# A hybrid attention layer on one core: the pace of the branch merges, a PSUM bank of the scan, and the order of the output phase

## The chip, the cores and the metric

The kernel runs on one core of one Trainium2 chip. The metric is the device time of one execution in microseconds; of several executions the median counts. The kernel before was timed three times: 2359.21, 2356.31 and 2359.18 us, median 2359.18 us. The five engines are named as in the profile: PE (TensorE, matmul), DVE (VectorE), ACT (ScalarE), POOL (GpSimd) and SP (SyncE, which here issues nearly all DMAs).

## The reference

One decoder layer for 2048 tokens of width 1024 in float32. The input is normalised and projected to 9224 columns. Branch A is a gated delta rule with 4 heads of 128 and chunks of 64; branch B is windowed attention in three groups of 4 heads, merged by the softmax denominators. Both are gated, projected back, mixed, multiplied by `w_out`, and x is added. Cut to what the change touches:

```python
tmat = lax.linalg.triangular_solve(eye + lower, ..., left_side=True, lower=True, unit_diagonal=True)
...
def step(S, inp):                      # scan over the 32 chunks, 4 heads
    v_new = ui - einsum('bhck,bhkv->bhcv', wi, S)
    o = einsum('bhck,bhkv->bhcv', qi * exp(gci), S) + einsum('bhij,bhjv->bhiv', ai, v_new)
    S = S * exp(glast) + einsum('bhck,bhcv->bhkv', ki * exp(glast - gci), v_new)
    return S, o
...
alpha = jax.nn.softmax(jnp.stack(lses, axis=0), axis=0)     # over the three groups
o_swa = jnp.sum(alpha[..., None] * jnp.stack(outs, axis=0), axis=0)
...
merged = sigmoid(g_dn) * y_dn + sigmoid(g_swa) * y_swa
x = x + merged @ w_out[layer]
```

## The kernel before

Large matmuls are done in float32 precision from two halves: each operand is split into a high part and a low remainder (`split`, L89 to L91: the high part on ACT, the remainder on DVE or POOL), and three products are added in one PSUM tile. Many of them are also done by a scheme of seven products for a 2x2 block product (`PROD`), for which sums of blocks are formed first.

The stages follow each other on PE. First comes the projection for the attention branch with the attention itself in its gaps. Then `cunits` (L710) runs 36 units of 128 output columns each, four tiles of 512 tokens to a unit, every tile 24 matmuls of 512 columns. Its units are three z units (branch A's gate), twelve units of the delta rule's q, k and v, twelve g units (the mixing gates, L1158), five z units (L1149) and four g units. Beside these units the delta rule's serial work is done:

- `inverse` (L1000) inverts 128 triangular 64x64 blocks at once, one block to a partition. Row i needs all rows before it: a product of i x i elements (L1023), two memsets, and a sum over the last axis (L1026), all on DVE. It starts in the first g unit.
- `combine` merges the three attention groups, 128 tokens at a time, 16 times (L1251). One merge is: a load of 128 x 1560 floats into an `oc` buffer; a minimum (L1260) and a difference (L1261) on DVE; an exp on ACT (L1262); four small operations on DVE (L1265 to L1268); three products of 512 columns on DVE (L1271); two additions on POOL (L1276); and a DMA to `osd` (L1278).
- `scan` (L1031) begins 20 steps after the inverse has ended. For each of 16 pairs of chunks it runs three stages for the heads 0, 1 (g = 0) and 2, 3 (g = 1). Stage 2 multiplies keys by new values into the tile `p4` (L1099 to L1101), from which DVE updates the states S (L1103).

After `cunits` come the branch projections and the mixing (`fin_y`, eight blocks of 256 tokens with eight tiles each), which writes `mscr`, and last the output phase: `group` (L1388), eight times, multiplies 256 tokens by `w_out` in seven products of 12 matmuls. Around them stand the loads of x (`x_load`), the holding of partial sums (`keep`, L1400 on ACT and L1402 on DVE), additions of x on POOL (`plus`, L1405), results with their DMA out (`result`, L1408 and L1409), and, for the operand four products ahead, loads from `mscr` (`m_load`, L1355), block sums (L1376) and splits (`m_op`).

Work that stands beside matmuls is placed by a clock of steps: `self.at(delay, fn)` puts a function on a list, and `hook()`, called after every second k (six matmuls of 512 columns in `cunits`, some 1.4 us), advances the clock by one and runs what is due. This sets the order in the program's source. What order an engine really gets is up to a planner: in a stretch under `pinned(False)` PE, ACT, DVE and POOL keep the source order and SP's is planned; under `pinned(True)` SP keeps it too; from the inverse's start to the end of `cunits` only PE keeps it; and in the output phase of the kernel before the planner orders all engines. Each engine runs its own queue strictly in the order it was given, and an instruction that waits holds up those behind it.

On-chip memory is drawn from pools, and a tile with `bufs=n` turns through n buffers: a new tile waits until the oldest one's users are done. PSUM has eight banks in these stages: three `mm`, two `tp`, two `sc`, one `po`. In the scan, stage 0 takes an `sc` tile for each pair of heads, the preparation of the next chunks two more, stage 1 a `tp` tile each, stage 2 the `po` tile twice. The gate tiles `gt` have two buffers in `cunits`, and a g tile is read out by ACT (L1161) and written to memory, a z tile by ACT (L1152) and DVE (L1153).

## Time and profile before

| What | Before |
|---|---|
| Median of 3 runs (lowest to highest) | 2359.18 us (2356.31 to 2359.21) |
| The profiled execution: its own time, its span | 2355.83 us, 2353.8 us |
| Granted TensorE clock, mean | 0.993 |
| PE, DVE, ACT, POOL busy | 2275.0, 1435.6, 919.8, 941.2 us |
| The inverse on DVE, from its first product to row 63's end | 1421.2 to 1694.8 us |
| First matmul of the scan | 1766.2 us |
| Output phase on PE | 2188.9 to 2350.0 us |

The profile is of one execution. Its span reaches from the first to the last instruction; the time of an execution has a little more around it (here 2.0 us). A row of a group names a source line, an engine, an operation, what it writes and reads, how often it ran, the busy time and mean duration, and the idle time just before it with the releaser of that wait. A row of the timeline gives start and duration in us. A row of the list of waits says which engine waited where, for whom, and then the total in us, the number of times and the longest.

### The profile page before, as it was taken

How to read it: one execution, taken by the hardware profiler on the slowest of the kernel's cores; microseconds unless marked ns; L12 is line 12 of the kernel's file. 1: busy time of each engine (PE TensorE's matmuls, PEld its weight loads, DVE VectorE, ACT ScalarE, POOL GpSimd, SP SyncE). 2: the span in 40 equal slices, each digit the busy share in tenths (PEclk: the TensorE clock that was granted, in tenths of full speed). 3: DMA queues.
4: the chain of work that ended last, by engine and by line, in shares of the span. 5: the costliest groups of instructions: out<-in, count | busy, mean ns of one | idle time of the engine just before them, and what ended most of it. 6: DMA issues, size and time to landing. Idle time of an engine off the chain costs nothing. (4 is left out here: it accounts for less than half of the span.)

```text
span 2353.8 us, 43662 instructions
## 1 busy us (share of the span) xinstructions
PE 2275.0 (97%) x15120; PEld 2063.3 (88%) x15120; DVE 1435.6 (61%) x2980; ACT 919.8 (39%) x2959; POOL 941.2 (40%) x1299
## 2 busy tenths in 40 slices
PE   7999999989999999999999999999999999999999
PEld 7999999889999999888788888777788888999787
DVE  6566586694445545446777768999813443666653
ACT  5345466653434435444666651111113333211221
POOL 6374265575303303303675563334212332332543
PEclk9999999999999999999999999999999999999999
DMA  9989889857887888853554445444345657787752
GB/s 304 325 279 322 276 276 292 271 160 247 259 258 239 250 272 262 257 145 98 127 131 123 117 108 181 144 127 134 126 143 164 196 170 229 232 277 240 249 157 89
DMA packets 557267, 485.80 MB, mean 206 GB/s; under 512 B 68280, under 2 KB 517112, under 8 KB 554104
## 3 DMA queue, kind: packets, MB, share of 16 engines
q1 hardware_dynamic: 556760, 482.95, 66.7%
q8 instruction: 120, 1.97, 0.3%
q14 instruction: 99, 0.81, 0.1%
q10 hardware_dynamic: 288, 0.07, 0.0%
HBM read 280.23 MB, written 202.67 MB: 205 GB/s over the span
## 5 line engine op out<-in xcount | busy, mean ns | idle before, releaser
L723 PE MATMUL mm<-hh,w 128*128 128x512 f32 x1152 | 465.2, 404 | 13.2 <-ACT gt L1161 9.8
L725 PE MATMUL mm<-hh,w 128*128 128x512 f32 x1152 | 458.2, 398 | 0.0
L724 PE MATMUL mm<-hl,w 128*128 128x512 f32 x1152 | 457.6, 397 | 0.0
L436 PE MATMUL mm<-w,hh 128*128 128x256 f32 x1760 | 326.8, 285 | 0.0
L723 PEld LDWEIGHTS mm<-hh,w 128*128 128x128 f32 x1152 | 220.8, 192 | 62.3 <-ACT gt L1161 12.9
L436 PEld LDWEIGHTS mm<-w,hh 128*128 128x128 f32 x1760 | 270.2, 189 | 0.0
L725 PEld LDWEIGHTS mm<-hh,w 128*128 128x128 f32 x1152 | 217.4, 189 | 46.9
L436 PE MATMUL mm<-hh 128*128 128x256 f32 x880 | 257.5, 293 | 0.0
L724 PEld LDWEIGHTS mm<-hl,w 128*128 128x128 f32 x1152 | 218.1, 189 | 41.9
L436 PE MATMUL mm<-hl,hh 128*128 128x256 f32 x880 | 249.7, 284 | 0.5 <-POOL hl L298 0.5
L436 PE MATMUL mm<-hh,hl 128*128 128x256 f32 x880 | 249.6, 284 | 0.0
L436 PE MATMUL mm<-w,hl 128*128 128x256 f32 x880 | 248.0, 282 | 0.0
L91 POOL TENSOR_TENSOR w<-raw,w 128x512 fp32r<-128x512 f32 x68 | 95.0, 1402 | 287.2 <-ACT w L90 281.8
L610 DVE CUSTOM_DVE_ANT_0 p<-sc,mask 128x128 f32<-128x128 f32 (+1 forms) x192 | 70.1, 365 | 214.6 <-PE sc L607 84.3
L436 PEld LDWEIGHTS mm<-hl,hh 128*128 128x128 f32 x880 | 169.1, 192 | 0.9 <-POOL hl L298 0.9
L436 PEld LDWEIGHTS mm<-hh 128*128 128x128 f32 x880 | 169.2, 192 | 0.0
L436 PEld LDWEIGHTS mm<-hh,hl 128*128 128x128 f32 x880 | 168.8, 192 | 0.0
L371 POOL TENSOR_SCALAR st<-st 128x4 f32<-128x4 f32 x96 | 21.4, 223 | 367.4 <-ACT junk L370 365.4
L436 PEld LDWEIGHTS mm<-w,hl 128*128 128x128 f32 x880 | 165.6, 188 | 0.0
L837 DVE SCALAR_TENSOR_TENSOR acc<-xr,cw,acc 128x512 f32<-128x512 f32 x144 | 121.2, 842 | 16.7 <-ACT acc L835 11.5
L594 ACT ACTIVATE kq<-tp 128x256 fp32r<-128x256 f32 x148 | 56.3, 381 | 179.7 <-PE tp L587 178.8
L1276 POOL TENSOR_TENSOR oc<-oc 128x512 f32<-128x512 f32 x32 | 62.2, 1943 | 131.3 <-DVE oc L1271 72.9
(351 smaller groups left out, 5798.8 us busy)
## 6 DMA issues: line engine op xcount, KB each, us to landing
wdr<-w SPq DMA_DIRECT2D x56, 512.0 KB, 4.8
w<-wdr SPq DMA_DIRECT2D x54, 512.0 KB, 4.8
qk<-qks SPq DMA_DIRECT2D x212, 128.0 KB, 4.0
qks<-rec SPq DMA_DIRECT2D x96, 256.0 KB, 3.1
raw<-in_w_in_dram SPq DMA_DIRECT2D x68, 256.0 KB, 3.2
gscr<-gt SPq DMA_DIRECT2D x64, 256.0 KB, 4.0
gt<-gscr SPq DMA_DIRECT2D x64, 256.0 KB, 4.6
wdr<-hh SPq DMA_DIRECT2D x28, 512.0 KB, 4.5
```

The costliest lines, as they stand in the source:

```text
L91: eng.tensor_tensor(out=l, in0=raw, in1=h.bitcast(F32), op=ALU.subtract)
L371: nc.gpsimd.tensor_scalar(out=st[:, 0:4], in0=st[:, 0:4], scalar1=1.0 / P, scalar2=EPS, op0=ALU.mult, op1=ALU.add)
L436: mm = lambda x, y, **kw: nc.tensor.matmul(o, x, y, skip_group_check=True, **kw)
L594: nc.scalar.activation(h, src, AF.Copy)
L610: nc.vector.tensor_tensor_reduce(out=p[:, lo:hi], in0=sc[:, lo:hi], in1=self.mask[:, slot * P + lo:slot * P + hi], scalar=3e38, scale=-SCA ...
L723: nc.tensor.matmul(pr, wh[:, k, :], a, start=(k == 0), stop=False)
L724: nc.tensor.matmul(pr, wh[:, k, :], b, start=False, stop=False)
L725: nc.tensor.matmul(pr, wl[:, k, :], a, start=False, stop=(k == KT - 1))
L837: nc.vector.scalar_tensor_tensor(out=acc, in0=xr[:, j:j + 512], scalar=w[:, j:j + 1], in1=acc, op0=ALU.mult, op1=ALU.add)
L1276: nc.gpsimd.tensor_tensor(out=o, in0=o, in1=oc[:, g, :, 0:P], op=ALU.add)
```

## The change

There are three parts.

The merges: the next merge starts six steps after the last instead of ten; there are three `oc` buffers instead of two, and a load is issued two merges ahead; the exp is placed one step after the minimum and the difference. The inverse's rows are paced with 0.97 in place of 0.95 (the sum of the 63 waits goes from 223 to 219 steps). The merges' pool is closed when the scan starts and not after `cunits`.

The scan: in stage 2 the tile `p4` of the heads 2, 3 is taken from the two `sc` banks; that of the heads 0, 1 stays in `po`.

The output phase: it runs under `pinned(True)`, so all engines and SP keep the source order. The first group's first two loads of x are issued earlier, after the sixth tile of the last block of `fin_y`, into the buffers `th` and `tl`, which are no longer used by then.

```diff
-            self.at(max(1, round((2 * i * i / 960.0 + 0.5) / 0.95)), lambda: row(i + 1))
+            self.at(max(1, round((2 * i * i / 960.0 + 0.5) / 0.97)), lambda: row(i + 1))
...
-                p4 = self.ps.tile([P, 512], F32, name="po", bufs=1)
+                p4 = self.ps.tile([P, 512], F32, name=("po", "sc")[g], bufs=1 + g)
...
     def comb_setup(self, M):
         self.M, self.ocs = M, {}
-        self.comb_load(0)
-        self.comb_load(1)
-        self.at(8, lambda: self.combine(0))
+        for t in (0, 1):
+            self.comb_load(t)
+        self.at(8, lambda: self.comb_next(0))
...
-        oc = self.ocs[t] = self.cb.tile([P, G, H, 130], F32, name="oc", bufs=2)
-        if t < 2:
+        oc = self.ocs[t] = self.cb.tile([P, G, H, 130], F32, name="oc", bufs=3)
+        if t < 3:
...
-    def combine(self, t):
-        nc, cb, V = self.nc, self.cb, self.nc.vector
-        oc = self.ocs.pop(t)
-        if 0 < t < 15:
-            self.comb_load(t + 1)
-        sm = cb.tile([P, 4, 12], F32, name="cs", bufs=2)
+    def comb_next(self, t):
+        if t < 14:
+            self.comb_load(t + 2)
+        self.combine(t, self.ocs.pop(t), self.cb.tile([P, 4, 12], F32, name="cs", bufs=2))
+        if t < 15:
+            self.at(6, lambda: self.comb_next(t + 1))
+
+
+    def combine(self, t, oc, sm):
...
-        nc.scalar.activation(e, e, AF.Exp)
...
+        self.at(1, lambda: nc.scalar.activation(e, e, AF.Exp))
         self.at(2, share)
         for g in range(G):
             self.at(3 + g, lambda g=g: weigh(g))
         for g in (1, 2):
             self.at(5 + g, lambda g=g: add(g))
-        if t < 15:
-            self.at(10, lambda: self.combine(t + 1))
...
+    def x_first(self):
+        self.x0 = []
+        for c, n in enumerate(("th", "tl")):
+            x = self.lp.tile([P, 4, P], F32R, name=n, bufs=1).bitcast(F32).rearrange("p a c -> p (a c)")
+            self.nc.sync.dma_start(x, dr(self.i["x"], c * 512, [[D, P], [1, 512]]))
+            self.x0.append(x)
+
     def group(self, g):
...
         def x_load(t, c):
+            if g == 0 and t == 0:
+                xo[t, c] = self.x0[c]
+                return
...
         def start_scan():
+            bst.close()
             ist.close()
...
         pin.close()
-        bst.close()
         cst.close()
...
+                    if nb == 7 and m == 5:
+                        self.x_first()
...
-        for g in range(8):
-            self.group(g)
-        self.flush()
+        with pinned(True):
+            for g in range(8):
+                self.group(g)
+            self.flush()
```

## The prediction

> **What bounds the kernel now.** I read the page's top lines first, then the list of what TensorE (PE) waited for (us in total, times, longest).

> ```profile
> span 2353.8 us, 43662 instructions
> PE 2275.0 (97%) x15120; PEld 2063.3 (88%) x15120; DVE 1435.6 (61%) x2980; ACT 919.8 (39%) x2959; POOL 941.2 (40%) x1299
> ```

> ```profile
> PE mm L723 <- ACT gt L1161: 9.8, 7, 2.9
> ...
> PE po L1101 <- DVE S L1103: 5.6, 16, 0.4
> ...
> PE mm L723 <- DVE M L1025: 3.5, 1, 3.5
> ```

> ```profile
> L1423 PE MATMUL mm<-hh 128*128 128x512 f32 x128 | 50.8, 397 | 4.6 <-ACT hold L1400 2.3 <-DVE hold L1408 1.9 <-DVE hold L1402 0.4
> ```

> PE is busy for 2275.0 of 2353.8 us, and the edit removes no matmul. It can therefore only touch PE's idle time, 78.8 us, and of that only what belongs to three stages: the inverse (9.8 + 3.5 = 13.3 us), the scan (5.6 us) and the output phase (the last row, a group of its matmuls: 4.6 us in three stops). The other waits of the list belong to stages that the diff doesn't touch. A fed matmul of 512 columns starts 0.23 us after the one before (the chain's row: 126.97 us for 552), while its record is 0.40 us long, so a stop of PE costs about 0.17 us more than its idle time shows.

> ```profile
> 2223.02 126.97 PE mm L1423 x552
> ```

> The same row, from the end of the chain of waits, says that from 2223 us PE runs without a gap to its last matmul: in the output phase only the first group and a half can give anything.

> **The scan: another bank for the second pair's product.** The timeline of one scan step (PE, DVE):

> ```profile
> 1887.77 0.61 PE L1101 MATMUL po<-vn,rec 128*128 128x128 f32 x4
> 1888.21 0.61 PE L1106 MATMUL tp<-vn,rec 128*128 128x128 f32 x4
> 1888.41 0.61 DVE L1103 SCALAR_TENSOR_TENSOR S<-S,eglb,po 128x128 f32<-128x128 f32 x2 [1.61 <-PE po L1101]
> 1889.16 0.68 PE L1101 MATMUL po<-vn,rec 128*128 128x128 f32 x4 [0.34 <-DVE S L1103]
> 1889.68 0.61 PE L1106 MATMUL tp<-vn,rec 128*128 128x128 f32 x4
> 1892.33 0.61 PE L1084 MATMUL sc<-S,rec 128*128 128x128 f32 x4
> ```

> The second pair's product (second L1101) waits until DVE has read the first pair's out of the only `po` bank. Four such matmuls fed without a stop take 1888.21 - 1887.77 = 0.44 us, so the second L1101 would have started at 1888.65; it started at 1889.16 (0.51 us lost) and then took 1889.68 - 1889.16 = 0.52 instead of 0.44 (0.08 more). That is 0.59 us a step, 16 steps: 9.4 us, against 5.6 by the idle column. With the product in one of the two `sc` banks, five tiles instead of four turn through `sc` in a step. The new one takes the bank of the second pair's L1084/L1086, read out two hook steps earlier. What is late next is the following step's L1084: it now needs the bank that DVE's second L1103 reads out. That L1103 would run right behind the matmul, ending near 1890.0 by the rows above, and L1084 would come at 1892.33 - 0.59 = 1891.74, so 1.7 us of cover; with the cover gone the wait returns at the same 0.5 us. I take **9.0 us** (bounds 0 and 9.4).

> **The inverse: merges at six hook steps, three buffers.** Here DVE's queue decides. First the window from the inverse's start to its end, with the busy times of PE, PE's weight loads, DVE, ACT and POOL, then DVE's and POOL's groups in it:

> ```profile
> 1421.00:1695.00 274.00, 261.15 (x1116) 211.26 (x1114) 264.91 (x401) 40.30 (x84) 96.68 (x54) 0.99 0.43 128
> ```

> ```profile
> L1023 DVE TENSOR_TENSOR Z<-M 128x1 f32<-128x1 f32 (+62 forms) x63 | 107.0, 1698 | 0.6
> L1026 DVE TENSOR_REDUCE M<-Z 128x1 f32<-128x1 f32 (+62 forms) x63 | 95.4, 1515 | 0.0
> L1271 DVE TENSOR_TENSOR oc<-oc,cs 128x512 f32<-128x512 f32 x48 | 36.4, 786 | 0.0
> L1261 DVE TENSOR_TENSOR cs<-cs,oc 128x12 f32<-128x12 f32 x16 | 9.7, 608 | 0.0
> L1265 DVE TENSOR_TENSOR cs<-cs,oc 128x12 f32<-128x12 f32 x16 | 8.6, 535 | 0.0
> ...
> L1260 DVE TENSOR_REDUCE cs<-oc 128x4 f32<-128x12 f32 x16 | 2.7, 171 | 6.6 <-DMA oc<-oscr 6.5
> ```

> ```profile
> L1276 POOL TENSOR_TENSOR oc<-oc 128x512 f32<-128x512 f32 x32 | 62.2, 1943 | 131.3 <-DVE oc L1271 72.9 <-DVE M L1024 57.0 <-DMA oc<-oscr 0.7
> L91 POOL TENSOR_TENSOR w<-raw,w 128x512 fp32r<-128x512 f32 x22 | 34.8, 1598 | 29.1 <-ACT w L90 23.9 <-PE mm L725 5.2
> ```

> DVE is busy 264.91 of 274.00 us: a serial chain of 63 rows with the merges in between. Moving merges forward removes none of this work. What the work's end holds up, and what the merges hold up:

> ```profile
> 1690.53 4.23 DVE L1026 TENSOR_REDUCE M<-Z 128x63 f32<-128x3969 f32 x1
> 1694.67 0.67 DVE L1153 SCALAR_TENSOR_TENSOR gt<-gt,mm 128x512 f32<-128x512 f32 x1
> ```

> ```profile
> 1695.40 0.80 PE L723 MATMUL mm<-hh,w 128*128 128x512 f32 x1 [3.47 <-DVE M L1025]
> ```

> ```profile
> ACT cs L1262 <- DVE cs L1261: 113.9, 15, 12.3
> ACT gt L1161 <- DMA gscr<-gt: 55.0, 11, 11.2
> ```

> The 9.8 us at `gt` have this cause: a merge's exp (L1262) stands in ACT's queue ahead of the next gate tiles and waits for a DVE operation that comes late, up to 12.3 us; three `mm` banks fill and PE stops. The 3.5 us are the first z tile's DVE operation (L1153), queued behind row 63. Had the seven stops not been, PE would have been at that same place about 11 us sooner (9.8 + 7 x 0.17) and would have waited those 11 us more, because row 63 ends when DVE's work ends. So the stage's loss, 13.3 + 8 x 0.17 = 14.7 us, is one loss. Ending the exps before the long rows moves the stops to the z tile; only an earlier end of row 63 takes them away. The third `oc` buffer lets a merge's load go out two merges ahead: it can remove DVE's 6.5 us on `oc<-oscr`, less some of it where the denser merges still outrun their loads and their `osd` writes. The exp's later step (+1), the pool closed at the scan's start, the third load's extra 128x1 copy and the row pace (waits of 219 instead of 223 steps, so the scan stands 4 x 1.4 = 5.6 us earlier in PE's order) cost nothing I can find: the scan's first matmul came long after its data were asked for.

> ```profile
> 1712.13 0.60 SPq L1050 DMA_DIRECT2D t<-tscr  x1
> ```

> ```profile
> 1766.18 0.68 PE L1062 MATMUL sc<-t,lo 64*64 64x64 f32 x8
> ```

> Fifty-four us lie between these; without that cover the scan would be late by what it was advanced, 5.6 us. I take **4 us** for the inverse; the bounds are all 14.7 us, and a loss worked out below.

> Against the merges speak collisions. L1261 took 0.17 or 1.26 us:

> ```profile
> 1552.40 0.17 DVE L1261 TENSOR_TENSOR cs<-cs,oc 128x12 f32<-128x12 f32 x1
> ...
> 1578.45 1.26 DVE L1261 TENSOR_TENSOR cs<-cs,oc 128x12 f32<-128x12 f32 x1
> ```

> By the means above, L1261 and L1265 lost 16 x (0.61 - 0.17) + 16 x (0.54 - 0.17) = 13 us; L1023 took 107.0 - 95.4 = 11.6 us more than L1026 over the same elements, at most that lost. That is about 25 us, or 23 delays of 1.26 - 0.17 = 1.09 us, against 32 + 22 = 54 POOL operations. In six steps, the next merge's L1261 falls on the step of the first add (+6) and its L1265 right after the second (+8 against +7). If all 54 cost one such delay, DVE loses 59 - 25 = 34 us. I expect a few more, 2 or 3 us, which is why 4 and not 6.5. [...]

> **The output phase in source order.** Timeline of SP, ACT, DVE and PE around the first group:

> ```profile
> 2188.91 0.39 PE L1423 MATMUL mm<-hh,oh 128*128 128x512 f32 x1
> ```

> ```profile
> 2193.11 0.39 SPq L1355 DMA_DIRECT2D o<-mscr  x1
> 2193.55 1.86 SPq L1395 DMA_DIRECT2D xo<-in_x_dram  x4
> 2195.45 1.23 SPq L1355 DMA_DIRECT2D mt<-mscr  x2
> ```

> ```profile
> 2197.33 0.63 ACT L90 ACTIVATE oh<-o 128x512 fp32r<-128x512 f32 x1 [4.76 <-PE mm L1423]
> 2203.76 0.63 ACT L90 ACTIVATE hh<-mt 128x512 fp32r<-128x512 f32 x1 [5.80 <-DMA mt<-mscr]
> ```

> ```profile
> 2199.38 0.69 DVE L1408 TENSOR_TENSOR xo<-mm,xo 128x512 f32<-128x512 f32 x1 [3.90 <-DMA xo<-in_x_dram]
> ...
> 2206.91 0.69 DVE L1408 TENSOR_TENSOR hold<-mm,hold 128x512 f32<-128x512 f32 x1
> ```

> Before, group 2's operand (`o`) was fetched and split ahead of group 1's (`mt`), whose load landed at 2203.76. In source order, two x loads (256 KB each) are issued in the last block before the phase (after its sixth tile, some 2 x 2.8 us before 2188.91), and group 2's loads (2 x 512 KB) come later; 1.5 MB leave the queue ahead of `mt`. At the 400 GB/s that the DMA engines reached there that is 3.8 us:

> ```profile
> GB/s 437 374 425 414 373 382 222 316 207 293 336 263 150 76 23 23 242 78 117 172 195 300 218 269 394 359 425 398 425 441 386 414 386 281 293 285 195 308 168 133
> ```

> So `mt` lands near 2200. The two x issues pass in front of SP's last three `mscr` writes (by 512 KB, 1.3 us); nobody reads those until the last group. Order now matters at one place: the hold of `u3` (L1402) stands on DVE behind the three operations of group 1's first operand (L91, L1376, L1376), and product 5 needs it. Products take 12 x 0.23 = 2.76 us, so product 5 is due at 2188.91 + 13.8 = 2202.7. From 2200: 0.63 (ACT) + 4 x 0.69 = 2203.4, a stop of 0.7 us. With `mt` as late as before: 2203.76 + 3.4 = 2207.2, a stop of 4.5, and nothing gained. The loss now is 4.6 + 3 x 0.17 = 5.1; I take **4 us** (bounds 0 and 5.1). In later groups SP issues the x loads at the group's head, 3 x 2.76 = 8.3 us before a result needs the first, and `mt` seven products (19 us) ahead; in the crowded first group landing took 5.8 (2193.55 to 2199.38) and 8.3 us (2195.45 to 2203.76), so both stay covered. Without that cover each group would stop PE by what its load is late.

> **Sum.** 9 + 4 + 4 = 17 us off the profiled execution: 2353.8 becomes 2336.8 and its own time, 2355.83, becomes 2338.8. That execution lies 3.35 us under the median of the runs, 2359.18, so the median goes to **2342 us**.

> **Rivals.**
> 1. The whole inverse stage clears (DVE's order puts the z tile's operation between the rows, or the rows end 15 us sooner): 14.7 instead of 4, 2331 us. For it: ACT's exps end with the short rows. Against: DVE's work stays the same.
> 2. The inverse gives nothing or takes back up to 13 us, because exps and `osd` writes hold ACT and SP up earlier instead: 2346 to 2359, typically 2350. For it: ACT already waited 113.9 us at these exps. Against: rows are shorter there.
> 3. The scan's wait only moves to the `sc` banks, so that part of the change does nothing: 2351. Against: 1.7 us of cover.
> 4. [...] If all 54 POOL operations delay DVE, row 63 ends 34 - 6.5 = 27.5 us later, and the z tile and PE with it: 2359.2 - 13 + 27.5 = 2374 us. It makes the kernel slower from 13 + 6.5 = 19.5 us of new delay, 18 collisions more than the 23. Against: POOL's operations are the same in number, and under half collided so far.

> **How the numbers follow.** The forecast holds 52% (its own range 2336 to 2348), rival 1 9%, rival 2 22%, rival 3 8%, rival 4 9%. The measurement can tell about 0.2% (4.7 us) from no change. The range 2330 to 2353 takes in the forecast, nearly all of rivals 1 and 3, and the better two thirds of rival 2: 81%. Faster by over 0.2% (under 2354.5): 52 + 9 + 16 + 7 = 84%; within 0.2%: 6 from rival 2 and 1 from rival 3, 7%; slower: 9%.

> **What would show it.** Scan right: no wait of L1101 on L1103, and 0.44 us between the second L1101 and its L1106. Inverse right: no DVE wait on `oc<-oscr`, the last exp near 1550, the seven stops at L1161 mostly gone, the z tile's wait longer than 3.5 us. Output right: `mt` before 2201 counted from the old start of the phase, waits of L1423 under 1 us. I am wrong if the z tile's wait vanishes with them (rival 1), if L1261 and L1265 average near 1 us (rival 4), or if PE stops anew in a stage after the scan.

## The result and the profile after

The changed kernel takes 2343.67 us (median of four, 2342.14 to 2347.07). The kernel before, timed beside it, takes 2357.74 us (2355.19 to 2359.21). The ratio is 0.9943, with a 95% interval of 0.9926 to 0.9961. Forecast were 2342 us with a range of 2330 to 2353. The total came out; the three terms behind it did not.

The top of the profile page after (span, then busy time, share and instructions of each engine):

```profile
span 2341.5 us, 43663 instructions
PE 2275.0 (97%) x15120; PEld 2065.6 (88%) x15120; DVE 1434.0 (61%) x2981; ACT 919.0 (39%) x2959; POOL 938.9 (40%) x1299
```

PE's busy time is the same 2275.0 us to the tenth, so all that was won is time in which PE stood still or ran slowly. The list of PE's waits after (total, times, longest):

```profile
PE mm L723 <- ACT gt L1161: 9.8, 5, 4.3
...
PE mm L723 <- DVE M L1025: 4.4, 1, 4.4
...
PE tp L1095 <- DVE rr L1088: 2.1, 3, 0.8
```

The sixteen waits of L1101 are gone. The gate tiles' wait has kept its 9.8 us, in five stops instead of seven, the z tile's wait has grown from 3.5 to 4.4 us, and L1095, in the scan, waits 2.1 us where before it waited 0.5. The end of the chain of waits after:

```profile
2183.66 154.07 PE mm L1435 x672
```

The output phase now runs without a gap from its first matmul to its last: 672 matmuls in 154.07 us, 0.23 us each.

(Lines 1251 to 1300 of the kernel before stand some three to twenty lines lower now: the minimum is L1264, the difference L1265, the exp L1282, the small operations L1268 to L1271, the products L1274, POOL's additions L1279; the output phase's matmul is L1435.)

Where the 12.3 us between the two spans came from can be read off the starts of the stages on PE in the two timelines (each boundary to within two matmuls, at the same place in every kernel):

| Stretch on PE | Before | After | Won |
|---|---|---|---|
| Start to the first g unit (in which the inverse starts) | 1395.25 | 1396.06 | -0.8 |
| First g unit to the scan's first matmul | 370.93 | 366.86 + 5.6 = 372.5 | -1.5 |
| Scan, first to last matmul | 177.08 | 171.64 | 5.4 |
| Rest of the units | 47.47 | 53.02 - 5.6 = 47.4 | 0.05 |
| `fin_y` | 198.06 | 195.81 | 2.25 |
| Output phase | 160.80 | 153.95 | 6.85 |

The 5.6 us are the 24 matmuls by which the scan stands earlier in PE's order (four steps of 1.4 us): they lie behind the scan's start after and ahead of it before. Forecast were 4 us for the inverse, 9 for the scan, nothing for `fin_y` and 4 for the output phase.

Each column is one execution, and stages without an edit differ too. Over the fourteen traces of this document the stretch to the first g unit is 1394.7 to 1402.1 us long, so the -0.8 says nothing. The stretch from there to the scan, with the 5.6 us allowed for, is 369.3 to 372.0 us in the five kernels with the old merges and 372.0 to 372.9 in the three with the new ones and no other edit there, so the -1.5 is a small loss at most. The old output phase is 159.7 to 160.8 us long, so the edit is worth 5.7 to 6.85 us there.

### The profile page after: what moved, and what is told of

The parts are those of the page before. It is cut to its first block, busy times and chain, and to the rows that moved or that the text cites. A ratio compares the mean times of both kernels' runs of the same rounds, so it can differ in the third digit from the quotient of the medians.

```text
span 2341.5 us, 43663 instructions
## 1 busy us (share of the span) xinstructions
PE 2275.0 (97%) x15120; PEld 2065.6 (88%) x15120; DVE 1434.0 (61%) x2981; ACT 919.0 (39%) x2959; POOL 938.9 (40%) x1299
## 5 line engine op out<-in xcount | busy, mean ns | idle before, releaser
L723 PE MATMUL mm<-hh,w 128*128 128x512 f32 x1152 | 465.4, 404 | 14.1 <-ACT gt L1161 9.8
L725 PE MATMUL mm<-hh,w 128*128 128x512 f32 x1152 | 458.9, 398 | 0.0
L723 PEld LDWEIGHTS mm<-hh,w 128*128 128x128 f32 x1152 | 220.9, 192 | 62.7 <-ACT gt L1161 12.0
L725 PEld LDWEIGHTS mm<-hh,w 128*128 128x128 f32 x1152 | 217.9, 189 | 47.4
L91 POOL TENSOR_TENSOR w<-raw,w 128x512 fp32r<-128x512 f32 x68 | 95.3, 1403 | 340.6 <-ACT w L90 340.4
L370 ACT ACTIVATE junk<-rec 128x128 f32<-128x128 f32 x288 | 89.4, 310 | 54.6 <-DVE rec L364 47.5
```

Of the source, the lines that this page charges most:

```text
L91: eng.tensor_tensor(out=l, in0=raw, in1=h.bitcast(F32), op=ALU.subtract)
L370: nc.scalar.activation(self.junk, src[:, j * P:(j + 1) * P], AF.Square, accum_out=st[:, j:j + 1])
L723: nc.tensor.matmul(pr, wh[:, k, :], a, start=(k == 0), stop=False)
L725: nc.tensor.matmul(pr, wl[:, k, :], a, start=False, stop=(k == KT - 1))
```

## The experiments

All ratios are to the kernel before, timed in the same series. Stage lengths are read as in the table above, from one profiled execution each, with the same 5.6 us allowed for where the scan stands earlier.

### The parts alone

Only the scan's bank:

```diff
-                p4 = self.ps.tile([P, 512], F32, name="po", bufs=1)
+                p4 = self.ps.tile([P, 512], F32, name=("po", "sc")[g], bufs=1 + g)
```

> The kernel before with the scan's edit alone (the second pair's product in an sc bank). Theory A, from the two traces: the wait of L1101 on L1103 goes (9.3 us of PE time), but PE then waits for L1088 at L1095, because L1088 stands on DVE behind L1122, which waits for POOL; that gives 3.8 us back, so 5 to 6 us faster than before. Theory B, the prediction's term: 9 us faster, with no new wait. If the edit only moved its wait: 0 us.

Measured: 2348.13 us, ratio 0.9962 (0.9947 to 0.9977). The scan is 170.76 us long (6.3 less), `fin_y` 196.32 (1.7 less). Of the stages without an edit, the output phase is 0.9 us shorter and the stretch to the first g unit 3 us longer.

Only the output phase:

```diff
+                    if nb == 7 and m == 5:
+                        self.x_first()
...
-        for g in range(8):
-            self.group(g)
-        self.flush()
+        with pinned(True):
+            for g in range(8):
+                self.group(g)
+            self.flush()
```

> The kernel before with the output phase's edit alone (source order, first x loads early). Theory A, from the two traces: the three stops of the phase's start go, worth 6.9 us of PE time, so 6 to 7 us faster, and the wait of 1.6 us at 2152 us, before this phase, stays. Theory B, the prediction's term: 4 us faster with a stop of about 1 us left. If the stop before the phase at 2152 us goes too, this part is worth 8 to 9 us.

Measured: 2351.37 us, 0.998 (0.9969 to 0.9991). The output phase is 153.95 us long, as in the full change.

Only the merges, with the rows' pace and the earlier closing of their pool:

```diff
-        self.at(8, lambda: self.combine(0))
+        self.at(8, lambda: self.comb_next(0))
...
-        oc = self.ocs[t] = self.cb.tile([P, G, H, 130], F32, name="oc", bufs=2)
+        oc = self.ocs[t] = self.cb.tile([P, G, H, 130], F32, name="oc", bufs=3)
...
+            self.at(6, lambda: self.comb_next(t + 1))
...
+        self.at(1, lambda: nc.scalar.activation(e, e, AF.Exp))
...
-            self.at(10, lambda: self.combine(t + 1))
```

> The kernel before with the inverse's edit alone (six steps, three buffers, exp a step later, row pace, pool closed early). Theory A: the stage's loss is one loss, set by the end of row 63; that end moved from 1694.8 to 1697.5 us between the two profiles, so this part is worth nothing: 0 to 3 us slower than before, L1161 stops near 10 us, z tile's stop 3 to 5 us. Theory B, the prediction's term: 4 us faster.

Measured: 2358.61 us, 1.0013 (1.0003 to 1.0024): by a hair slower. The trace is of the slowest of its twelve executions (2364.31 us), so its stages are read and not its total. The list of PE's waits in the stretch from the first g unit to the scan:

```profile
PE mm L723 <- ACT gt L1161: 8.0, 4, 3.1
PE mm L723 <- DVE M L1025: 4.4, 1, 4.4
```

That is 12.4 us of waiting against 13.3 before, and still the stretch is 372.9 us long against 370.9. Less idle time and a longer stage do not go together unless PE also runs more slowly; the last section returns to this.

The scan and the output phase, without the merges (both diffs above together):

```diff
+                p4 = self.ps.tile([P, 512], F32, name=("po", "sc")[g], bufs=1 + g)
...
+        with pinned(True):
```

> The scan's and the output phase's edits without the merges'. Theory A: 5.5 + 6.9 us faster than before, 12 to 15 us with the stop at 2152 us, so as fast as the changed kernel (2343.7 us, 14 us faster) or up to 2 us faster than it. Theory B: 13 us faster, the changed kernel 4 us faster than this one.

Measured: 2343.27 us, 0.9945 (0.9932 to 0.9958), which is the full change's 0.9943. The merges' part contributes nothing that can be measured; what it does alone points to the slower side.

### The output phase: order or early loads

The kernel before with the source order, but without the two early loads of x:

```diff
-        for g in range(8):
-            self.group(g)
-        self.flush()
+        with pinned(True):
+            for g in range(8):
+                self.group(g)
+            self.flush()
```

> The kernel before with the output phase in source order, without the early x loads. The first group then loads four x blocks ahead of group 1's operand. Theory A, by the prediction's working: that operand lands 1.3 us later than with the early loads, and the first result waits on DVE for its x block, so a stop of 2 to 5 us stays at the phase's start: 2 to 5 us faster than before. Rival B: the source order alone does it, 6 to 7 us off the phase as with both.

Measured: 2352.62 us, 0.9989 (0.998 to 0.9998); the output phase is 155.40 us long. The group of its matmuls that has a wait (count, busy time, mean, idle time before it):

```profile
L1423 PE MATMUL mm<-hh 128*128 128x512 f32 x128 | 49.9, 390 | 1.2 <-ACT hh L90 1.2
```

The order alone turns three stops of 4.6 us into one of 1.2 us, at the split of `mt`, and gives 5.4 of the 6.85 us. The early loads take the other 1.45 us away. In the changed kernel the split of `mt` on ACT stands here:

```profile
2193.72 0.63 ACT L90 ACTIVATE hh<-mt 128x512 fp32r<-128x512 f32 x1 [5.53 <-DMA mt<-mscr]
```

The phase starts at 2183.50 instead of 2188.91, so on the old clock this is 2199.1, against 2203.76 before.

### The scan: what is late next

One step of the scan after, PE's timeline:

```profile
1880.56 0.60 PE L1101 MATMUL po<-vn,rec 128*128 128x128 f32 x4
1881.00 0.61 PE L1106 MATMUL tp<-vn,rec 128*128 128x128 f32 x4
1881.45 0.61 PE L1101 MATMUL sc<-vn,rec 128*128 128x128 f32 x4
1881.90 0.61 PE L1106 MATMUL tp<-vn,rec 128*128 128x128 f32 x4
...
1884.54 0.60 PE L1084 MATMUL sc<-S,rec 128*128 128x128 f32 x4
...
1887.72 1.23 PE L1095 MATMUL tp<-rr,vb 128*128 128x128 f32 x8
```

The four groups of four now follow each other every 0.45 us, as forecast, and L1084 comes without a wait. But L1095 takes 1.23 us instead of the 1.05 us that it took in the same step before:

```profile
1895.49 1.05 PE L1095 MATMUL tp<-rr,vb 128*128 128x128 f32 x8
```

DVE's rows ahead of it, after, and then before:

```profile
1886.88 0.48 DVE L1122 TENSOR_SCALAR os<-qs,oss 128x128 f32<-128x128 f32 x2 [1.85 <-POOL oss L1120]
1887.28 1.12 DVE L1088 SCALAR_TENSOR_TENSOR rr<-sc,ksn,rec 128x128 f32<-128x128 f32 x4
```

```profile
1894.10 0.48 DVE L1122 TENSOR_SCALAR os<-qs,oss 128x128 f32<-128x128 f32 x2 [1.85 <-POOL oss L1120]
1894.50 1.12 DVE L1088 SCALAR_TENSOR_TENSOR rr<-sc,ksn,rec 128x128 f32<-128x128 f32 x4
```

L1088 makes L1095's operand and stands on DVE behind the scaling L1122, which waits for a chain of small POOL operations. Counted from the first L1101, L1122 starts 1886.88 - 1880.56 = 6.32 us later after, and 1894.10 - 1887.77 = 6.33 us before: the POOL chain hangs on the first pair and did not move. PE, relieved of its 0.59 us, now comes to L1095 sooner than that chain ends. The experiment moves the scaling from DVE's queue to POOL's, so that L1088 has nothing that waits ahead of it:

```diff
-                    nc.vector.tensor_scalar(out=os[:, sl(j)], in0=o[:, sl(j)], scalar1=ss[:, 6 + j:7 + j], scalar2=None,
-                                            op0=ALU.mult)
+                    G.tensor_scalar(out=os[:, sl(j)], in0=o[:, sl(j)], scalar1=ss[:, 6 + j:7 + j], scalar2=None,
+                                    op0=ALU.mult)
```

> The changed kernel with the scan's output scaling (L1122) on POOL instead of DVE, so that L1088 on DVE no longer stands behind an operation that waits for POOL's chain. Theory A: the waits of L1095 on L1088 go, and the 3.8 us of PE time that the scan's edit gave back return: 3 to 5 us faster than the changed kernel. Rival B: L1088 is late because DVE is full there, and the waits stay: within 1 us of the changed kernel.

Measured: 2341.09 us, 0.9935 (0.9922 to 0.9948). The scan is 167.30 us long, 4.3 us less than after, and the waits at L1095 are gone. DVE's row shows why: L1088 waits for PE now.

```profile
1887.12 0.61 DVE L1088 SCALAR_TENSOR_TENSOR rr<-sc,ksn,rec 128x128 f32<-128x128 f32 x2 [2.50 <-PE sc L1086]
```

The whole kernel's time does not tell the two apart (the intervals overlap); the stage's length does.

### The inverse: the z tile, ACT's order

First the changed kernel with the z tiles two units later, so that PE comes to the first of them when row 63 is done:

```diff
-        self.ccols = zc[:3] + dc + gc[:12] + zc[3:] + gc[12:]
+        self.ccols = zc[:3] + dc + gc[:14] + zc[3:] + gc[14:]
...
-        self.cunits(zu[:3] + du + gu[:12] + zu[3:] + gu[12:], {3: open_dn, 15: lambda: self.at(9, start_inverse)}, tail)
+        self.cunits(zu[:3] + du + gu[:14] + zu[3:] + gu[14:], {3: open_dn, 15: lambda: self.at(9, start_inverse)}, tail)
```

> The changed kernel with the five z units two units (44 us) later: two more g units stand between. Row 63 then ends (1697.5 us) before the first z tile is due. Theory A (one loss, set by row 63's end, paid in advance by the exps' stops): the z tile's stop of 4.4 us goes, the stops at L1161 (9.8 us) stay, since g tiles still stand behind exps; 4 to 6 us faster than the changed kernel. Rival B (the z tile's stop is a fixed wait for the inverse that any unit after it pays): no difference.

Measured: 2337.65 us, 0.9923 (0.9911 to 0.9936). The list of PE's waits in the stretch:

```profile
PE mm L723 <- ACT gt L1161: 8.6, 4, 3.1
```

The z tile's wait has gone and did not come back in this stretch, which is 7.5 us shorter than after (359.33 against 366.86), though the wait was only 4.4 us. Of these the scan gives 2.4 us back (174.02 against 171.64): PE waits 3.2 us at L1095 there in place of 2.1; one of these stops is 1.5 us long, with a stretch at half clock behind it (granted clock 0.50 from 1893.1 to 1896.5 us). The stops at the gate tiles are a loss of their own: without a wait for row 63 behind them they still cost.

Next the changed kernel with ACT, too, in source order from the inverse's start to the scan's, so that no exp would be put ahead of a gate tile that is ready sooner:

```diff
-            pin.enter_context(tc.manual_schedule(engines={E.PE}))
+            pin.enter_context(tc.manual_schedule(engines={E.PE, E.Activation}))
```

> The changed kernel with ACT, too, in source order from the inverse's start to the scan's start, so that no exp stands ahead of a gate tile that is due before it. Theory A (one loss): the stops at L1161 fall from 9.8 to at most 2 us, and the z tile's stop grows from 4.4 to 11 to 14 us; in all within 3 us of the changed kernel. Rival B (the exps' stops are a loss of their own): L1161's stops go, the z tile's stays at 4.4 us; 9 to 11 us faster than the changed kernel.

Measured: 2349.47 us, 0.9976 (0.9967 to 0.9985). The edit did not do what it was meant to. ACT's waits at the exp after, then with this edit, and then PE's waits with it:

```profile
ACT cs L1282 <- DVE cs L1265: 88.7, 12, 10.0
...
ACT cs L1282 <- DVE M L1024: 23.1, 3, 12.5
```

```profile
ACT cs L1282 <- DVE cs L1265: 123.7, 15, 15.0
```

```profile
PE mm L723 <- ACT w L90: 9.5, 3, 6.3
...
PE mm L723 <- ACT gt L1161: 4.2, 3, 1.6
```

In source order, too, the exps wait for a late DVE, 123.7 us at fifteen exps in place of 88.7 + 23.1 = 111.8, and what stands behind them now is the split of the weights, so PE stops there. Neither expectation came true. With both edits together,

```diff
+            pin.enter_context(tc.manual_schedule(engines={E.PE, E.Activation}))
...
+        self.ccols = zc[:3] + dc + gc[:14] + zc[3:] + gc[14:]
```

> Both edits together: ACT in source order and the z units two units later. Theory A (one loss): with no gate tile behind an exp and no z tile behind row 63 the whole loss of the stage goes, 12 to 16 us faster than the changed kernel, about 2330 us. Rival B: 9 to 11 us from the exps, none from the z units. If the loss only moves on to the scan's start (its data come from row 63): 0 to 5 us.

the time is 2352.36 us, 0.9985 (0.9975 to 0.9995), with nearly the same stops as in ACT's order alone. Source order on ACT does not mend a DVE that is late; other orders of its queue were not tried.

### The inverse: why DVE is late

Around the longest stop at a gate tile after, 4.26 us, DVE's timeline:

```profile
1545.11 3.17 DVE L1023 TENSOR_TENSOR Z<-M 128x1849 f32<-128x1849 f32 x1
1548.20 1.25 DVE L1268 TENSOR_TENSOR cs<-cs,oc 128x12 f32<-128x12 f32 x1
...
1551.56 0.16 DVE L1265 TENSOR_TENSOR cs<-cs,oc 128x12 f32<-128x12 f32 x1
1551.64 2.16 DVE L1023 TENSOR_TENSOR Z<-M 128x1936 f32<-128x1936 f32 x1
```

then ACT's and PE's:

```profile
1551.76 0.21 ACT L1282 ACTIVATE cs<-cs 128x12 f32<-128x12 f32 x1 [9.17 <-DVE cs L1265]
1551.87 0.61 ACT L90 ACTIVATE w<-raw 128x512 fp32r<-128x512 f32 x1
1552.39 1.09 ACT L1161 ACTIVATE gt<-mm 128x512 f32<-128x512 f32 x2
```

```profile
1553.02 0.79 PE L723 MATMUL mm<-hh,w 128*128 128x512 f32 x1 [4.26 <-ACT gt L1161]
```

The product over 1849 elements took 3.17 us, the next one over 1936 only 2.16; a product of twelve elements took 1.25 us instead of 0.16. Taken at the pace of the next product and at 0.16 us, some 1.1 + 1.1 us were lost ahead of one difference (L1265), the exp waits for it on ACT, and a weight split, two gate tiles and PE wait behind the exp. That is read from the order of the rows. Both DVE operations started while POOL's two additions (L1279) ran, from 1544.66 to 1549.41 us, and the small one ended 0.04 us after them. Two experiments test it and take these additions away. The first leaves out POOL's 32 additions, and with them the merging of groups 1 and 2 (only group 0's share is written out):

```diff
-            nc.gpsimd.tensor_tensor(out=o, in0=o, in1=oc[:, g, :, 0:P], op=ALU.add)
+            pass
```

> The changed kernel without POOL's 32 additions of the merges: only the first group's share of the merged attention is written out, all else stays. It prices the collisions of DVE and POOL. Theory A: L1274, L1268, L1271 and L1265 fall to their undisturbed 0.69 and 0.17 us, some 15 us of DVE time, row 63 ends 10 to 17 us earlier and the stage's loss of 14.2 us falls to 0 to 4 us: 10 to 14 us faster than the changed kernel. Rival B (the loss comes from the exps' place in ACT's queue, not from DVE's amount of work): the stops at L1161 stay above 7 us, less than 6 us faster.

Measured: 2324.79 us, 0.987 (0.9857 to 0.9884). From the first g unit to the scan 345.95 us, 20.9 less than after, and PE waits nowhere in it. DVE's groups from the inverse's start on, after and then without the additions:

```profile
L1023 DVE TENSOR_TENSOR Z<-M 128x1 f32<-128x1 f32 (+62 forms) x63 | 109.4, 1736 | 1.1
...
L1274 DVE TENSOR_TENSOR oc<-oc,cs 128x512 f32<-128x512 f32 x48 | 41.6, 892 | 0.1
L1268 DVE TENSOR_TENSOR cs<-cs,oc 128x12 f32<-128x12 f32 x16 | 9.0, 572 | 0.0
...
L1264 DVE TENSOR_REDUCE cs<-oc 128x4 f32<-128x12 f32 x16 | 2.6, 163 | 2.8 <-DMA oc<-oscr 2.8
```

```profile
L1023 DVE TENSOR_TENSOR Z<-M 128x1 f32<-128x1 f32 (+62 forms) x63 | 101.7, 1614 | 1.1
...
L1274 DVE TENSOR_TENSOR oc<-oc,cs 128x512 f32<-128x512 f32 x48 | 35.2, 757 | 0.0
...
L1268 DVE TENSOR_TENSOR cs<-cs,oc 128x12 f32<-128x12 f32 x16 | 4.8, 303 | 0.0
```

The three rows alone fall by 7.7 + 6.4 + 4.2 = 18.3 us, and row 63 ends 279.8 instead of 301.5 us after the first g unit, 21.7 us sooner. That is more than the 10 to 17 us expected. So one addition on POOL puts off the end of DVE's rows by 21.7 / 32 = 0.68 us in the mean, beside the 1.88 us that it takes on POOL.

The second experiment keeps the result: a group's product and its addition become one instruction on DVE, four of 128 columns for each of groups 1 and 2, and POOL adds nothing.

```diff
-            nc.gpsimd.tensor_tensor(out=o, in0=o, in1=oc[:, g, :, 0:P], op=ALU.add)
+            if g == 0:
+                V.tensor_tensor(out=o, in0=o, in1=c[:, 0, :].unsqueeze(2).to_broadcast([P, n, P]), op=ALU.mult)
+            else:
+                for h in range(n):
+                    V.scalar_tensor_tensor(out=oc[:, 0, h, 0:P], in0=oc[:, g, h, 0:P], scalar=c[:, g, h:h + 1],
+                                           in1=oc[:, 0, h, 0:P], op0=ALU.mult, op1=ALU.add)
```

> The changed kernel with each merge's second and third product joined with its addition on DVE (four operations of 128 columns each), and no addition on POOL: the same result. Without the additions row 63 ended 21.7 us earlier after the inverse's start; the eight short operations in place of two long ones cost DVE about 0.9 us a merge (8 x 0.28 less 2 x 0.69), 14 us in all. Theory A (the collisions with POOL set the stage's loss): row 63 ends 5 to 9 us earlier, 5 to 9 us faster than the changed kernel. Rival B (it is the amount of DVE work, and the joined operations collide with POOL's splits as well): within 3 us of it or slower.

Measured: 2327.68 us, 0.9877 (0.9863 to 0.989). PE waits nowhere from the first g unit to the scan, 346.31 us. DVE's groups:

```profile
L1023 DVE TENSOR_TENSOR Z<-M 128x1 f32<-128x1 f32 (+62 forms) x63 | 100.7, 1599 | 1.0
...
L1279 DVE SCALAR_TENSOR_TENSOR oc<-oc,cs 128x128 f32<-128x128 f32 x128 | 39.4, 366 | 0.0
L1276 DVE TENSOR_TENSOR oc<-oc,cs 128x512 f32<-128x512 f32 x16 | 13.6, 851 | 0.0
```

DVE does the additions as well, 39.4 + 13.6 = 53.0 us in place of 41.6, and gets 8.7 us back at L1023 alone. Row 63 ends only 3.9 us sooner (297.6 us after the first g unit), and yet both the stops at the gate tiles and the z tile's wait are gone. Both expectations missed this: Theory A had a gain of 5 to 9 us, and it is about 16. DVE's timeline at the last rows shows where the z tile's operation (L1153) now stands; below it the changed kernel's:

```profile
1673.88 4.16 DVE L1023 TENSOR_TENSOR Z<-M 128x3844 f32<-128x3844 f32 x1
1677.96 0.68 DVE L1153 SCALAR_TENSOR_TENSOR gt<-gt,mm 128x512 f32<-128x512 f32 x1
...
1688.36 4.22 DVE L1026 TENSOR_REDUCE M<-Z 128x63 f32<-128x3969 f32 x1
```

```profile
1693.31 4.23 DVE L1026 TENSOR_REDUCE M<-Z 128x63 f32<-128x3969 f32 x1
1697.45 0.67 DVE L1153 SCALAR_TENSOR_TENSOR gt<-gt,mm 128x512 f32<-128x512 f32 x1
```

The z tile's operation stands inside row 62 instead of behind row 63, 18.4 us sooner counted from the first g unit (282.9 us after it against 301.4). It is the planner that put it there; why it did so with this merge and not with the other, no run shows. The planner also gave ACT's queue another order: the exps wait 81.2 us at thirteen places in place of 111.8 at fifteen. How much of the relief at the gate tiles comes from a DVE that is less late and how much from this order, no run separates. Both experiments that take the additions off POOL are free of stops.

Last, the fused merge with the z tiles two units later and the scan's scaling on POOL:

```diff
+                    G.tensor_scalar(out=os[:, sl(j)], in0=o[:, sl(j)], scalar1=ss[:, 6 + j:7 + j], scalar2=None,
...
+        self.ccols = zc[:3] + dc + gc[:14] + zc[3:] + gc[14:]
...
+                    V.scalar_tensor_tensor(out=oc[:, 0, h, 0:P], in0=oc[:, g, h, 0:P], scalar=c[:, g, h:h + 1],
```

> The joined merges, the z units two units later and the scaling on POOL, all in the changed kernel. If the three add up: 6 (z later) + 5 to 9 (joined) + 3 to 5 (scaling), but the first two pay for the same loss, 14 to 15 us at most: 14 to 19 us faster than the changed kernel, about 2327 us. If the loss only moves: 6 to 10 us.

Measured: 2320.66 us, 0.9847 (0.9833 to 0.986): faster than both kernels, 35 us under the one before and some 23 under the change. The stretch to the scan is 345.95 us (346.31 with the fused merge alone, so the later z tiles add almost nothing once there is no wait), the scan 166.85.

## Why the prediction was right, and where it was wrong

**The total.** The sum went by 17 us and the trace shows 12.3: 9 became 5.4, 4 became -1.5, 4 became 6.85, and 2.25 us came from `fin_y` and -0.8 from the stages ahead, for which nothing was forecast. The errors have both signs, so the forecast of 2342 us lies closer to 2343.67 than its terms deserve: that the total came out so well is in good part luck.

**The scan: mechanism right, the next wait wrong.** That 0.59 us a step goes was right; L1101 no longer waits, and from the first pair's L1101 to the second L1106 it is 1881.90 - 1880.56 = 1.34 us in place of 1.91. The step that failed is "What is late next is the following step's L1084". L1084 had its cover. Late next was L1095, behind L1088, behind L1122 and a POOL chain that the edit did not shorten; moving L1122 alone gave 4.3 us back. The two DVE rows that show it were in the trace of before: L1122 waited 1.85 us with L1088 right behind it. Looking only at the bank that the edit touches, I did not follow the next operand on the other engines.

**The inverse: rival 2, nothing gained.** Four of its steps can be judged. That moving the merges only moves the stops held: the 9.8 us stayed, and the z tile's wait grew, as forecast (4.4). The third `oc` buffer took 3.7 of the 6.5 us on `oc<-oscr`, not all (2.8 remain), and the last exp came at 1573.7, not near 1550. Collisions did rise by "a few more": the products of 512 columns went from 36.4 to 41.6 us, L1023 from 107.0 to 109.4 and the last small product (L1268 before, L1271 after) from 2.7 to 4.3, while the two small operations L1261 and L1265 of before fell from 18.3 to 13.5 us (a mean of 0.29 and 0.57 us, far from the 1 us that would have spoken for rival 4). That is about 4.5 us more in all against the 2 or 3 expected, and row 63 ended 301.5 us after the first g unit instead of 299.5. The step that failed as a statement is "only an earlier end of row 63 takes them away" and, with it, that all stops are "one loss". The fused merge took them all away with row 63 only 3.9 us sooner, the z tile's wait by the mechanism of rival 1 (its operation between the rows), and the later z tiles took one away and left the others. Rival 1's mechanism exists; this edit did not set it off. Rival 4's collisions exist too: the additions put row 63 off by 21.7 us. But most of that was there before, since the edit added only some 4.5 us.

**The output phase: right, the term mis-sized.** The stop of 0.7 us that was left in my reckoning did not come, since `mt` was split at 2199.1 on the old clock, a little ahead of the 2200 assumed; the three stops are gone. What went with them was 6.85 us where I had set 5.1 at most. The size of a stop was wrong, and that is the term behind the whole prediction: "a stop of PE costs about 0.17 us more than its idle time shows". The last section gives what it leaves out. With it the loss of the inverse before is 19.0 us and not 14.7.

**`fin_y`** is shorter in every kernel that has the scan's edit (195.7 to 196.9 us in ten) than in any that lacks it (197.6 to 198.7 in four). In the kernel before PE waits 4.0 us in it, in four stops; the longest is this one, in DVE's and PE's rows:

```profile
2149.94 0.75 DVE L1311 SCALAR_TENSOR_TENSOR z<-tp,dnw,z 128x512 f32<-128x512 f32 x1 [3.04 <-DMA z<-zscr]
...
2154.02 0.35 PE L1341 MATMUL mm<-oh,hh 128*128 128x256 f32 x1 [1.60 <-DVE gt L1345]
```

With the scan's edit alone the same DVE operation waits 1.02 us, and PE does not stop there:

```profile
2144.11 0.75 DVE L1311 SCALAR_TENSOR_TENSOR z<-tp,dnw,z 128x512 f32<-128x512 f32 x1 [1.02 <-DMA z<-zscr]
```

From the issue of the two loads of z (L1303) to this operation it is 2149.94 - 2144.84 = 5.10 us before and 2144.11 - 2141.01 = 3.10 us with the scan's edit alone: a load lands 2 us sooner after its issue. Why it does, with the same instructions in the same order, stays open.

## What to carry to other kernels

When a wait is removed, follow the operands of the next instructions on all engines, not only the buffer that was freed: here the next late one was a queue away and could be read in the trace of before. A sharing of work between DVE and POOL has to be priced with what POOL's instruction costs DVE (0.68 us for each addition of 128x512 here); doing the addition inside a DVE instruction brought the ratio from 0.9943 to 0.9877, though the changed order of the queues may have had a part in that. And where an engine waits for a late one, an order that puts other work ahead of the wait can help (two more units ahead of the z tiles took their wait away), and one that doesn't moves the stop (source order on ACT). The largest gain here came with taking POOL's additions away from beside the late engine.

## What the runs showed of the hardware

**A stop of PE can cost a stretch at half clock.** Behind the second stop in the output phase of the kernel before, the windows of 1 us and PE's timeline (start, duration) read:

```profile
2220.00:2221.00 1.00, 1.00 (x4) 0.81 (x3) 1.00 (x2) 0.00 (x0) 1.00 (x1) 0.50 0.01 4
2221.00:2222.00 1.00, 1.00 (x3) 0.72 (x3) 1.00 (x2) 0.00 (x0) 0.22 (x1) 0.50 0.00 0
```

```profile
2219.45 0.39 PE L1423 MATMUL mm<-hl,hh 128*128 128x512 f32 x1
...
2220.30 0.63 PE L1423 MATMUL mm<-hl,hh 128*128 128x512 f32 x1
2220.72 0.63 PE L1423 MATMUL mm<-hh,hl 128*128 128x512 f32 x1
```

The granted clock (third column from the right of the windows) is 0.50, and the matmuls start 0.42 us apart instead of 0.23. Summed over windows of half a microsecond, 1 minus the granted clock gives what such a stretch costs: 1.71 us where the whole of it falls on matmuls, so it lasts 3.4 us. With this third term the stages' losses close. The loss measured is the stage's length less that of a kernel in which PE does not wait there (the fused merge's 346.31 us, the changed kernel's output phase):

| Stage, kernel | Idle | Stops x 0.17 | Half clock | Sum | Measured |
|---|---|---|---|---|---|
| Inverse, before | 13.3 | 1.4 | 4.3 | 19.0 | 370.93 - 5.6 - 346.31 = 19.0 |
| Inverse, after | 14.2 | 1.0 | 5.6 | 20.8 | 20.6 |
| Inverse, merges alone | 12.4 | 0.9 | 7.7 | 21.0 | 21.0 |
| Inverse, z tiles later | 8.6 | 0.7 | 3.4 | 12.7 | 13.0 |
| Output phase, before | 4.6 | 0.5 | 1.7 | 6.8 | 6.85 |

So the merges alone made PE wait 0.9 us less and lose 3.4 us more to the clock, which is how a stage with less idle time became longer. In the traces of before and after, up to PE's last matmul, every such stretch (granted clock 0.50) lasts 3.41 us or two or three times that (6.83 and 10.24). The length of a stop alone does not tell whether one follows: in the fourteen traces, from the first g unit on, the shortest stop that was followed by a half-clock stretch is one of 1.47 us (in the scan with the z tiles later), and one of 3.47 us was followed by none.

| PE idle in a window at full clock | Windows | The next one at half clock |
|---|---|---|
| 1.86 us or more | 30 | 30 |
| 1.69 to 1.84 us | 8 | 2 |
| 1.65 us or less | 3794 | 1 (1.47 us idle, in a scan) |

In the kernel before the windows ahead of its three stretches hold 2.35, 2.37 and 1.88 us of idle time. In these traces a little over half a window of idle time is enough, and it is the idle time within one window that counts, not the length of a stop. The stop of 3.47 us that no such stretch followed (with the output phase's edit alone) lies across a boundary, 1.63 us in one window and 1.84 in the next. No run places a stop on purpose, and why the windows between 1.69 and 1.84 us differ stays open.

**A collision of DVE and POOL lasted until POOL's operation ended.** In the kernel before, L1261 took about 0.17 us eight times, 1.26 to 1.28 us five times, and 0.31, 0.72 and 0.97 us once each. Each L1261 and L1265 there that took more than 0.4 us, thirteen in all, started while an operation of POOL was running, an addition or a split, and ended within 0.05 us of that operation's end. The prediction put what all 54 POOL operations cost DVE at about 25 us; without the 32 additions row 63 ends 21.7 us sooner.
